# Low parts of weight chunks on GpSimd: four subtractions of 256 columns instead of one of 1024

## The chip, the cores and the metric

The kernel runs on one core of one Trainium2 chip. The metric is the device time of one execution in microseconds (us). The core has engines that run side by side, each with its own queue of instructions: TensorE (PE, with its weight loads shown as PEld), VectorE (DVE), ScalarE (ACT), GpSimd (POOL), and SyncE (SP), which here issues the loads.

## The reference

Two transformer-like layers follow each other on 256 tokens of width 2048, in float32. What matters here is the first one: a normed input is multiplied by a wide weight matrix, its columns feed three branches (a banded attention, a recurrent branch, an attention over a memory), and the branches are gated, projected and added.

```python
h = rms_norm(x, norm_g)
proj = h @ w_in
(aq, ak, av, az, br, bk, bv, bz, bwd, bad, cq, cz, ga, gb, gc) = jnp.split(proj, offsets, axis=-1)
ya = chunked_band_attention(aq, ak, av, a_rel_bias) * jax.nn.silu(az)
yb = rwkv7_time_mix(br, bk, bv, bwd, bad, ...) * jax.nn.silu(bz)
m = rms_norm(mem, mem_norm_g)
mk, mv = jnp.split(m @ w_mem_kv, 2, axis=-1)
yc = memory_cross_attention(cq, mk, mv) * jax.nn.silu(cz)
merged = sigmoid(ga) * (ya @ w_up_a) + sigmoid(gb) * (yb @ w_up_b) + sigmoid(gc) * (yc @ w_up_c)
x = x + merged @ w_o
```

The second layer has the same shape (attention, gated linear attention, a short convolution) and ends in a feed-forward block of width 5632.

## The kernel before

Each large product is done in split form. A weight chunk `w` of 128 partitions by 1024 columns (512 KB) is loaded by SP; ScalarE writes its rounded high part `wh` (line 163); the low part `wl = w - wh` is written by one subtraction of 1024 columns, on GpSimd or on VectorE (line 167). The activations lie as high and low parts too. `gemm_B` multiplies eight slices of 128 columns of each chunk: per slice one matmul of `wh` with 512 columns of activations and one of `wl` with 256 columns. `gemm_A` uses the chunk the other way round, as two slices of 512 columns, each read by two matmuls with `wl` and four with `wh`. There are four `w` buffers, three of `wh` and three of `wl`.

Which engine makes `wl` is a counter's doing. `share[0]` starts at 0.0 (all on VectorE, while the memory's keys and values are made), is 0.7 from line 334 to line 765 (seven of ten on GpSimd: the rest of the first layer up to the end of its branches), and is 0.0 again for all that follows. So GpSimd makes 161 chunks, all of 1024 columns, whose starts lie between 105.3 and 941.7 us; VectorE makes the other 802.

In that stretch TensorE works on two things at once: the weight products (the normed input against `w1A` and `w1B`), and the small matmuls of the recurrent branch (tiles `pk`, `G`, `Z`, `D`, `ch`, `oT`, `ptk`) and of the attentions (`sc`, `pt`, `po`). Between these small matmuls lie chains of short VectorE, ScalarE and GpSimd instructions of 256 columns or so: in `rwkv_inputs` the inverse square root (lines 242 to 244), `kk` (498), `k` (501), `t` (503) and the block-diagonal copies (508 to 513); in `rwkv_inverse` `lt`, `tt`, `Z`; in `rwkv_chain` `X` (599), `U` (602) and `S` (613); in the softmax `tp` (653); in the gates 669 and 677. GpSimd itself does a few of them (lines 482, 511, 514, 536, 538, 612, 633). At the end of the stretch the branch outputs `raw` are split into `yhl` by 24 pairs of instructions (lines 218 and 219, called from line 767).

The order of the instructions on each engine's queue is fixed when the kernel is built. The framework (`TileContext(nc, schedule_with_timeline_sim=True)`) chooses it by playing the program through with its own estimates of each instruction's duration, so a changed instruction can change the order around it. `rwkv_inputs`, `rwkv_inverse`, `rwkv_chain` and the fillers (the gates, the attention heads, the merge gates done ahead) are written in an order by hand, which this planner follows as their inputs allow.

Of the kernel before, what the change touches and what calls it, by code (L numbers as in the profile page):

```python
# [8 lines left out]
F32 = mybir.dt.float32  # L9
# [91 lines left out]
def _body(tc, a, out):  # L101
    nc = tc.nc
# [53 lines left out]
    share = [0.0]  # L156
    turn = [0]

    def wchunk(src, nel):
        w = wp.tile([128, 1024], F32, tag="w", name="w")  # L160
        nc.sync.dma_start(w[:, :nel], src)
        wh = whp.tile([128, 1024], F32R, tag="wh", name="wh")
        nc.scalar.copy(wh[:, :nel], w[:, :nel])  # L163
        wl = wlp.tile([128, 1024], F32R, tag="wl", name="wl")
        turn[0] += 1
        eng = nc.gpsimd if turn[0] * share[0] % 1.0 < share[0] else nc.vector
        eng.tensor_sub(wl[:, :nel], w[:, :nel], wh[:, :nel].bitcast(F32))  # L167
        return wh, wl

    def gemm_B(wd, act, kt=KD, m=128):  # L170

        ps = psg.tile([128, 512], F32, tag="g", name="g")
        for k0, kn in (chunks(kt) if m == 128 else [(0, kt)]):
            src = wd[128 * k0 * m:128 * (k0 + kn) * m].rearrange("(p c) -> p c", p=128)
            wh, wl = wchunk(src, kn * m)
            for j in range(kn):
                k = k0 + j
                mm(ps[:m, :], wh[:, j * m:(j + 1) * m], act[:, k, :], start=(k == 0), stop=False)
                mm(ps[:m, 256:512], wl[:, j * m:(j + 1) * m], act[:, k, 0:256], start=False, stop=(k == kt - 1))
        return ps  # L180

    def gemm_A(wd, act, kt=KD, ahead=None):

        ps = [psg.tile([128, 512], F32, tag="g", name="g") for _ in range(2)]
        for k0 in range(0, kt, 2):
            if ahead:
                ahead(k0)
            src = wd[128 * k0 * 512:128 * (k0 + 2) * 512].rearrange("(p c) -> p c", p=128)
            wh, wl = wchunk(src, 1024)
            for j in range(2):  # L190
                k = k0 + j
                for tt in range(2):
                    hi = act[:, k, tt * 128:(tt + 1) * 128]
                    lo = act[:, k, 256 + tt * 128:256 + (tt + 1) * 128]
                    h_ = wh[:, j * 512:(j + 1) * 512]
                    l_ = wl[:, j * 512:(j + 1) * 512]
                    mm(ps[tt], hi, h_, start=(k == 0), stop=False)
                    mm(ps[tt], hi, l_, start=False, stop=False)
                    mm(ps[tt], lo, h_, start=False, stop=(k == kt - 1))
        return ps  # L200
# [658 lines left out]
    for h in range(4):  # L859
# [23 lines left out]
        for cp in range(2):  # L883
            sl = slice(cp * 128, cp * 128 + 128)
# [176 lines left out]
```

## Time and profile before

| | |
|---|---|
| Time, median of 3 runs | 2996.11 us (2993.2 to 2996.36) |
| The profiled execution | 2997.74 us |
| Its span, first to last instruction | 2996.0 us |
| Mean granted TensorE clock | 0.992 of full speed |
| TensorE busy | 2935.0 us, 98% of the span |
| VectorE busy | 1966.4 us, 66% |
| ScalarE busy | 1439.8 us, 48% |
| GpSimd busy | 591.8 us, 20% |

The span is what the rows below cover; 1.74 us of the profiled execution lie around it. "Busy" is time with at least one instruction in work on that engine; an instruction that has been started and is held up counts as busy too.

### The profile page before, as it was taken

The numbers are of one execution on the slowest core, as the hardware profiler recorded it, in microseconds if no ns is written. First come the engines' busy times: TensorE is split into PE (matmuls) and PEld (weight loads), VectorE is DVE, ScalarE is ACT, GpSimd is POOL, SyncE is SP. The second block draws the span as 40 slices with busy tenths as digits, with TensorE's granted clock in tenths as the row PEclk, the third lists the DMA queues.
The fourth block names the chain that finished last, engine by engine and source line by source line (L and its number), as shares of the span: only waits on it lengthen the run. The fifth ranks groups of instructions, "written<-read, shape, count | busy, mean of one in ns | idle before, by whom it ended". The sixth has DMA issues, their size and how long they took to land.

```text
span 2996.0 us, 43985 instructions
## 1 busy us (share of the span) xinstructions
PE 2935.0 (98%) x16704; PEld 2575.3 (86%) x16704; DVE 1966.4 (66%) x3086; ACT 1439.8 (48%) x2174; POOL 591.8 (20%) x441
## 2 busy tenths in 40 slices
PE   8999999999999999999999999999999999999998
PEld 6888788888887888888888888888888888888887
DVE  6655687767656755666766776666676666666554
ACT  5544454444445544555445444444555444444443
POOL 6465455555564100100000000000000000000000
PEclk9999999999999999999999999999999999999999
DMA  7643233434345655665454555555555555555664
GB/s 254 198 145 133 97 117 132 142 127 135 125 150 188 222 190 190 204 198 173 153 168 164 189 190 190 190 190 190 184 196 188 190 191 191 190 190 186 189 189 148
DMA packets 151252, 522.42 MB, mean 174 GB/s; under 512 B 17200, under 2 KB 22320, under 8 KB 151040
## 3 DMA queue, kind: packets, MB, share of 16 engines
q1 hardware_dynamic: 148208, 512.72, 52.4%
q0 software_dynamic: 1824, 4.98, 0.4%
q8 instruction: 131, 2.15, 0.3%
q10 hardware_dynamic: 1008, 1.90, 0.2%
q14 instruction: 81, 0.66, 0.1%
HBM read 514.56 MB, written 4.98 MB: 173 GB/s over the span
## 4 chain that ended last, share of the span: by engine, by line
PE 81%; DVE 5%; issue 1%; ACT 1%; POOL 1%; DVEq 0%; ACTq 0%; POOLq 0%
PE g L153 76%; PE ch L153 1%; PE G L153 1%; PE oT L153 1%; POOL wl L167 1%; PE D L153 1%; PE Z L153 0%; DVE tt L568 0%; DVE wl L167 0%; PE po L153 0%; PE sc L153 0%; DVE tA L241 0%; PE glo L153 0%; DVE atrt L508 0%; DVE raw L677 0%
## 5 line engine op out<-in xcount | busy, mean ns | idle before, releaser
L153 PE MATMUL g<-xg,wh 128*128 128x512 f32 x4640 | 1636.2, 393 | 1.2 <-ACT wh L163 1.2
L163 ACT CAST wh<-w 128x1024 fp32r<-128x1024 f32 (+1 forms) x963 | 1004.3, 1043 | 1270.7 <-PE g L153 673.9
L167 DVE TENSOR_TENSOR wl<-w,wh 128x1024 fp32r<-128x1024 f32 (+1 forms) x802 | 983.1, 1226 | 718.4 <-ACT wh L163 716.5
L153 PE MATMUL g<-xg,wl 128*128 128x256 f32 x4640 | 1319.9, 285 | 6.5 <-POOL wl L167 6.5
L153 PEld LDWEIGHTS g<-xg,wh 128*128 128x128 f32 x4640 | 872.3, 188 | 179.6 <-ACT wh L163 1.8
L153 PEld LDWEIGHTS g<-xg,wl 128*128 128x128 f32 x4640 | 877.6, 189 | 9.6 <-POOL wl L167 7.4
L167 POOL TENSOR_TENSOR wl<-w,wh 128x1024 fp32r<-128x1024 f32 x161 | 395.5, 2460 | 233.2 <-ACT wh L163 212.6
L153 PE MATMUL g<-yhl,wh 128*128 128x512 f32 x768 | 269.8, 390 | 0.0
L153 PE MATMUL g<-wh,xg 128*128 128x512 f32 x768 | 250.9, 402 | 0.4 <-ACT va L318 0.4
L153 PE MATMUL g<-act,wh 128*128 128x512 f32 x704 | 244.1, 390 | 0.0
L153 PE MATMUL g<-yhl,wl 128*128 128x256 f32 x768 | 216.6, 282 | 0.0
L153 PE MATMUL g<-act,wl 128*128 128x256 f32 x704 | 198.5, 282 | 0.0
L785 POOL TENSOR_TENSOR accm<-accm,z 128x256 f32<-128x256 f32 x64 | 52.5, 820 | 654.1 <-DVE z L784 654.1
L153 PEld LDWEIGHTS g<-yhl,wh 128*128 128x128 f32 x768 | 144.2, 188 | 30.9 <-issue 0.3
L153 PEld LDWEIGHTS g<-wh,xg 128*128 128x128 f32 x768 | 143.8, 189 | 31.1 <-ACT va L318 0.5
L204 ACT COPY et<-g 128x256 f32<-128x256 f32 (+1 forms) x434 | 158.3, 365 | 6.4 <-PE g L153 6.4
L153 PE MATMUL g<-wl,xg 128*128 128x512 f32 x384 | 156.3, 407 | 1.6 <-DVE wl L167 1.6
L153 PEld LDWEIGHTS g<-act,wh 128*128 128x128 f32 x704 | 132.2, 188 | 27.7
L153 PEld LDWEIGHTS g<-yhl,wl 128*128 128x128 f32 x768 | 145.2, 189 | 0.0
L153 PEld LDWEIGHTS g<-act,wl 128*128 128x128 f32 x704 | 133.1, 189 | 0.0
L207 DVE TENSOR_TENSOR z<-g,et 128x256 f32<-128x256 f32 x216 | 90.4, 418 | 21.5 <-ACT et L204 21.0
L153 PE MATMUL g<-wh,mem_hl 128*128 128x512 f32 x256 | 84.2, 411 | 7.7 <-ACT wh L163 7.7
(348 smaller groups left out, 2964.0 us busy)
## 6 DMA issues: line engine op xcount, KB each, us to landing
w<-w2B SPq DMA_DIRECT2D x208, 512.0 KB, 3.4
w<-w1B SPq DMA_DIRECT2D x194, 512.0 KB, 3.5
w<-w_gate SPq DMA_DIRECT2D x88, 512.0 KB, 3.3
w<-w_ffup SPq DMA_DIRECT2D x88, 512.0 KB, 3.3
w<-w1A SPq DMA_DIRECT2D x64, 512.0 KB, 3.3
w<-w_down SPq DMA_DIRECT2D x64, 448.0 KB, 3.4
w<-w_mem SPq DMA_DIRECT2D x32, 512.0 KB, 4.5
w<-w_o SPq DMA_DIRECT2D x32, 512.0 KB, 4.3
```

Of the source, the lines that this page charges most:

```text
L153: nc.tensor.matmul(dst, lhsT=lhsT, rhs=rhs, start=start, stop=stop)
L163: nc.scalar.copy(wh[:, :nel], w[:, :nel])
L167: eng.tensor_sub(wl[:, :nel], w[:, :nel], wh[:, :nel].bitcast(F32))
L204: nc.scalar.copy(t[:m], ps[:m, 256:512])
L207: nc.vector.tensor_add(z[:m], ps[:m, 0:256], t[:m])
L785: nc.gpsimd.tensor_add(accm, accm, u)
```

## The change

The subtraction of a chunk that goes to GpSimd is cut into pieces of 256 columns, four instructions for 1024 columns. Chunks that go to VectorE stay as they were, and so does the count that picks the engine.

```diff
         turn[0] += 1
-        eng = nc.gpsimd if turn[0] * share[0] % 1.0 < share[0] else nc.vector
-        eng.tensor_sub(wl[:, :nel], w[:, :nel], wh[:, :nel].bitcast(F32))
+        if turn[0] * share[0] % 1.0 < share[0]:
+            for c in range(0, nel, 256):
+                sl = slice(c, c + 256)
+                nc.gpsimd.tensor_sub(wl[:, sl], w[:, sl], wh[:, sl].bitcast(F32))
+        else:
+            nc.vector.tensor_sub(wl[:, :nel], w[:, :nel], wh[:, :nel].bitcast(F32))
         return wh, wl
```

## Rows read from the trace of the kernel before

**Rows 1.** The page's first part: busy time, share of the span, instructions.

```profile
PE 2935.0 (98%) x16704; PEld 2575.3 (86%) x16704; DVE 1966.4 (66%) x3086; ACT 1439.8 (48%) x2174; POOL 591.8 (20%) x441
```

**Rows 2.** Windows: PE, PEld, DVE, ACT, POOL busy; clock, DMA share, GB/s.

```profile
75.00:950.00 875.00, 840.02 (x4836) 734.28 (x4836) 593.48 (x1082) 396.31 (x608) 481.95 (x300) 0.98 0.42 139
950.00:2996.00 2046.00, 2031.56 (x11622) 1791.82 (x11621) 1324.88 (x1942) 1001.17 (x1500) 63.35 (x91) 1.00 0.57 187
```

**Rows 3.** Waits of PE, 75 to 950 us: total, times, longest.

```profile
PE pk L153 <- DVE t L503: 8.3, 6, 3.6
PE g L153 <- POOL wl L167: 6.5, 3, 5.3
PE ch L153 <- DVE U L602: 4.1, 2, 3.4
...
PE g L153 <- ACT wh L163: 1.2, 1, 1.2
PE ch L153 <- DVE S L613: 1.1, 1, 1.1
```

**Rows 4.** Timeline around 843 us, POOL, DVE and PE: start, duration.

```profile
842.58 2.41 POOL L167 TENSOR_TENSOR wl<-w,wh 128x1024 fp32r<-128x1024 f32 x1
...
842.70 2.38 DVE L653 TENSOR_SCALAR tp<-tp,sm 128x128 f32<-128x128 f32 x1
...
845.14 0.44 PE L150 MATMUL pt<-con,tp 128*128 128x128 f32 x2 [1.38 <-DVE tp L653]
```

**Rows 5.** Timeline around 916 us, POOL and DVE.

```profile
915.75 2.41 POOL L167 TENSOR_TENSOR wl<-w,wh 128x1024 fp32r<-128x1024 f32 x1
...
918.11 2.60 POOL L167 TENSOR_TENSOR wl<-w,wh 128x1024 fp32r<-128x1024 f32 x1
...
915.78 2.65 DVE L669 SCALAR_TENSOR_TENSOR z<-et,z 128x256 f32<-128x256 f32 x1 [0.49 <-ACT et L668]
```

**Rows 6.** Groups of DVE by shape, 75 to 950 us.

```profile
L222 DVE SCALAR_TENSOR_TENSOR xg<-ld,par,xg 128x256 fp32r<-128x256 f32 x16 | 6.8, 482 | 0.0
```

**Rows 7.** Groups of POOL by shape: busy us, mean ns, idle before.

```profile
L167 POOL TENSOR_TENSOR wl<-w,wh 128x1024 fp32r<-128x1024 f32 x161 | 395.5, 2460 | 233.2 <-ACT wh L163 212.6 <-issue 7.5 <-PE G L153 6.6
...
L536 POOL TENSOR_TENSOR lt<-lt,con 128x256 f32<-128x256 f32 x16 | 11.8, 735 | 27.4 <-DVE lt L533 27.4
```

**Rows 8.** Timeline around 24 us, POOL and DVE, POOL in short instructions.

```profile
23.30 0.92 POOL L293 TENSOR_TENSOR acc<-acc,sq 128x256 f32<-128x256 f32 x1
24.18 0.79 POOL L289 TENSOR_TENSOR sq<-ld 128x256 f32<-128x256 f32 x1
24.94 1.71 POOL L293 TENSOR_TENSOR acc<-acc,sq 128x256 f32<-128x256 f32 x1
...
23.54 0.96 DVE L222 SCALAR_TENSOR_TENSOR mem_hl<-ld,par,mem_hl 128x256 fp32r<-128x256 f32 x1
24.43 1.63 DVE L167 TENSOR_TENSOR wl<-w,wh 128x1024 fp32r<-128x1024 f32 x1
```

**Rows 9.** Timeline around 280 us, POOL, DVE and PE.

```profile
278.77 2.52 POOL L167 TENSOR_TENSOR wl<-w,wh 128x1024 fp32r<-128x1024 f32 x1
...
279.01 2.99 DVE L513 TENSOR_TENSOR kt_d<-k,cum 64x256 f32<-64x256 f32 x2
...
283.27 0.49 PE L153 MATMUL ch<-btok 128*128 128x128 f32 x1 [3.42 <-DVE U L602]
```

**Rows 10.** Windows, all engines as in rows 2, after a long wait.

```profile
369.40:374.00 4.60, 4.60 (x15) 4.27 (x16) 4.48 (x12) 0.00 (x0) 1.47 (x4) 0.50 0.42 143
```

**Rows 11.** Waits of the load queue on SP.

```profile
SPq L161 <- POOL wl L167: 595.6, 152, 16.2
```

**Rows 12.** Windows, tile wl alone: PE, PEld, DVE, POOL busy; clock, DMA.

```profile
800.00:900.00 100.00, 62.18 (x216) 40.65 (x215) 6.10 (x5) 52.14 (x23) 1.00 0.47 149
```

**Rows 13.** Timeline around 924 us, POOL and DVE.

```profile
923.82 5.75 POOL L167 TENSOR_TENSOR wl<-w,wh 128x1024 fp32r<-128x1024 f32 x1 [3.11 <-ACT wh L163]
...
920.92 6.45 DVE L219 TENSOR_TENSOR yhl<-raw,yhl 128x256 fp32r<-128x256 f32 x19
```

## The prediction

> **What bounds the kernel now.** I read the busy times first: TensorE works in 98% of the span, GpSimd in little of it [rows 1]. So a gain can come only from time in which TensorE stands still or runs slowly, and the windows say where that is: from 950 us on it stands still for 2046 - 2031.6 = 14 us in 2046 at clock 1.00, between 75 and 950 us for 875 - 840 = 35 us at a mean clock of 0.98 [rows 2]. All 161 chunks made by GpSimd lie in that second stretch, so the change touches the right one, and the most that it could give back there is 35 us of waits and what the lower clock costs, at most 0.02 x 875 = 17.5 us.
>
> Third, the waits of TensorE in that stretch. Two reasons make up almost all of the 35 us: ten rows in which it waits for a VectorE instruction (from 8.3 down to 1.1 us, 26.7 together), and one in which it waits for `wl` from GpSimd (6.5 us in three waits, the longest 5.3) [rows 3].
>
> Fourth, the timeline around these waits, to see why VectorE is late. At 842.70 a VectorE instruction on 128 columns takes 2.38 us; it ends 0.09 us after a GpSimd subtraction of 1024 columns that began just before it, and TensorE starts on its result right behind it, after 1.38 us of standing still [rows 4]. At 915.78 the same: 2.65 us, ending 0.27 us after the subtraction [rows 5]. While GpSimd runs a chunk, a VectorE instruction that reads SBUF stands until the end of it. An instruction of twice that width takes 0.48 us when left alone [rows 6].
>
> **The change, part by part.**
>
> *1. Shorter holds: VectorE gets in between.* What an instruction of 256 columns on GpSimd takes is shown: 0.735 us, against 2.46 for 1024 [rows 7]. Whether VectorE gets its turn between two GpSimd instructions that follow each other at once is shown too: of the two chunks at 915.75 and 918.11 the second is recorded as started before the first has ended, yet the VectorE instruction at 915.78 is done at 918.43, and the second chunk takes 2.60 instead of 2.41 [rows 5]. And where GpSimd already works in instructions of 256 columns, the two engines take turns: at 23.30 and 24.18 GpSimd needs 0.92 and 0.79 us, and the VectorE instruction at 23.54 needs 0.96 [rows 8], where the same form alone needs 0.48 [rows 6]. So a VectorE instruction that meets quarters is held up by about 0.96 - 0.48 = 0.5 us, each time, instead of once per chunk for 1.9 to 2.2 us (2.38 and 2.65 less 0.48 [rows 4 to 6]), say 2.0.
>
> That splits the 26.7 us in two. Where one VectorE instruction stood in the way (`tp`, `tt`, `X`, `Z`, `raw` and others, eight rows, 26.7 - 8.3 - 4.1 = 14.3 us), 2.0 becomes 0.5, a saving of three quarters: 10.7 us. Where TensorE waits at the end of a long run of such instructions, the run meets every quarter: at 279.01 four copies of the lines 513 and 512 stood in front of `U`, the first two taking 2.99 us, 2.0 more than twice 0.48 [rows 6, 9]; with quarters each of the four is held for 0.5, which is 2.0, the same. The rows of `t` and `U` (12.4 us) are mostly such runs. I take 15% of them, 1.9 us; bounds are nothing, and three quarters (9.3).
>
> *2. The first quarter is there sooner.* The first matmul with `wl` needs the first 128 columns alone, there after 0.735 us instead of 2.46 [rows 7]: 1.7 us sooner. Of the three waits for `wl` the long one (5.3) gives 1.7, the other two (1.2 together) all they have: 2.9 us. No row shows that the framework lets a matmul start on a part of a tile that four instructions write; if it holds it until all is written, `wl` is ready after 4 x 0.735 = 2.94 us, 0.48 later than now, and this term becomes a loss of 3 x 0.48 = 1.4.
>
> *3. The clock.* Behind the long waits the granted clock is at the lower of its two levels: behind the longest wait for `t` (3.6 us [rows 3]) it was 0.50, which is 1.2 GHz, from 369.4 to 374 us [rows 10], a loss of 2.3 us. Up to 17.5 us go that way in the stretch [rows 2]. The longest waits (3.6, 5.3) get shorter but don't all vanish, so I take a third: 6 us, bounds nothing and 17.5.
>
> *4. What it costs.* Each chunk now keeps GpSimd for 4 x 0.735 = 2.94 us, 0.48 more; 161 chunks make 77 us [rows 7]. GpSimd is busy for 482 of the 875 us [rows 2], so the 393 idle ones take it. But 300 - 161 = 139 other GpSimd instructions stand in the same queue [rows 2, 7] (`kk` of line 511, `lt`, `tt`, `Sd`, `raw`, all links of the recurrent branch), and where one is behind a chunk it comes 0.48 us later. Chunks hold GpSimd for 395.5 of 875 us [rows 2, 7], 0.45, so it is 139 x 0.45 x 0.48 = 30 us of lateness over all these links. TensorE has other matmuls to do in most of that time, so I charge a third, 10 us; bounds are nothing and 30.
>
> "GPSIMD Engine Reference" in the Trainium skill, section "Instruction dispatch", speaks against small instructions: each pays a software dispatch of some tens of cycles. Taking 50 cycles of 1.2 GHz, three more per chunk would be an estimated 0.125 us, 20 us over all instead of the 77 that the rows give, and term 4 would shrink in that proportion from 10 to 2.6 us, the sum below from -11.5 to -18.9. The sum goes by the rows.
>
> The buffer `w` is also released later by the same 0.48 us, and SP's loads wait for that 152 times, 595.6 us in all [rows 11]. This costs nothing as long as the load has slack; the cover is that TensorE's waits for `wh`, which the loads feed, come to 1.2 us in the stretch [rows 3]. A wait of the load that grew by 0.48 us 152 times would be 73 us without this cover.
>
> *5. The order of the queues.* 483 more instructions go through the planner, which may put the small matmuls and their chains elsewhere, on any engine. No row prices that. The 35 us of waits are the outcome of one such order in some twenty places; I take nothing, with a bound of a quarter of it, 9 us, to either side.
>
> **The sum.** -10.7 - 1.9 - 2.9 - 6 + 10 = -11.5 us. The profiled execution took 2997.74 us, so 2986.2; the median of the runs lies 1.6 us below it, so 2984.6 against 2996.1. A measurement of this kernel tells about 0.2%, 6 us, from no change.
>
> **Rivals.**
>
> *All runs are long ones.* If VectorE always has the next instruction ready when a quarter ends, it is held four times for 0.5 us instead of once for 2.0, and nothing is won in term 1 or of the clock. For it speaks the place at 279 [rows 9], against it the place at 843, where one instruction stands between GpSimd and TensorE [rows 4]. Then 15% of 26.7, 4.0, and 2.9 of `wl` stand against a cost between nothing and 10: -7 to +3, or 2989 to 2999, around 2994.
>
> *GpSimd becomes the bound (slower).* Taking turns costs GpSimd too: a quarter takes 0.92 us beside an instruction of 256 columns, and 1.71 beside one of 1024 [rows 8]. Three and one of these are 4.5 us per chunk. Between 800 and 900 us GpSimd makes 23 chunks [rows 12], and its other instructions need (482 - 395.5)/875, a tenth of the time [rows 2, 7]; so above 90/23 = 3.9 us per chunk from its first start to its last end, TensorE waits for `wl`. At 4.5 it is 23 x 4.5 + 10 - 100 = 13 us late in that stretch, and with 3 us won elsewhere the time is 3006. A burst of VectorE can do the same to a quarter: at 923.82 a chunk stood for 3.3 us while 19 subtractions of line 219 ran without giving way [rows 13], and a chunk in quarters can be cut off by such a run in its middle. Against it: quarters without company make 2.94 us.
>
> *No handover between quarters (slower).* If the four run as one hold, VectorE stands for 2.94 instead of 2.46, a fifth longer: 0.2 x 26.7 = 5 us more, and 2.9 less for `wl`: with some of term 4, around 3003. The pair at 915.75 speaks against it [rows 5].
>
> *More than I think.* All eight rows vanish and most of the clock comes back: -14.3 - 6.5 - 12 + 6 = -27, 2969.
>
> **How the numbers follow.** The forecast gets 0.50 (its own range 2975 to 2992), the larger gain 0.11, all long runs 0.20, GpSimd as the bound 0.13, no handover 0.06. The range leaves out the larger half of the slow cases and what is beyond the large gain: 2968 to 3004. Faster by over 0.2% (under 2990): most of the forecast (0.47), the larger gain (0.11), a little of the long runs (0.03): 0.61. Slower by over 0.2% (over 3002): 0.11 of GpSimd as the bound, 0.04 of no handover, 0.03 from a worse order: 0.18. The rest is 0.21.
>
> **What would show it.** VectorE groups of the stretch whose means are now lifted by single long holds should drop towards 0.42 to 0.96 us, with none above 2 us. TensorE's waits for VectorE should fall from 26.7 to about 14, its idle time in the stretch from 35 to about 20, and the mean clock rise. The quarters should take 0.73 to 0.95 us, GpSimd's busy time in the stretch some 77 us more. The prediction is wrong if quarters run without VectorE in between, if TensorE waits for `wl` more than now, if the new order opens waits elsewhere, or if long runs are held for as much as before.

## The result and the profile after

The changed kernel takes 2968.03 us (median of 4 runs, 2967.79 to 2969.45) against 2996.11 before: 28.1 us less, a ratio of 0.9908 [0.9897, 0.992]. That lies 0.03 us inside the low end of the forecast's range, and 16.6 us under the forecast itself.

The page's first part, for the row of [rows 1]:

```profile
span 2966.1 us, 44553 instructions
PE 2923.9 (99%) x16704; PEld 2569.2 (87%) x16704; DVE 1933.4 (65%) x3086; ACT 1440.7 (49%) x2174; POOL 684.7 (23%) x924
```

The span fell from 2996.0 to 2966.1, by 29.9 us. TensorE's busy time fell by 2935.0 - 2923.9 = 11.1 us for the same 16704 matmuls, so those ran faster; what is left, 18.8 us, is standing still: 61.0 us before, 42.2 after. VectorE's busy time fell by 33 us for the same 3086 instructions, and GpSimd's rose by 93. The mean granted clock rose from 0.992 to 0.995, which is worth some 0.003 x 2980 = 9 of the 11.1 us (with three digits, give or take 3).

Windows, columns as in [rows 2] (the second ends with the shorter span):

```profile
75.00:950.00 875.00, 859.38 (x5006) 754.35 (x5005) 580.27 (x1111) 413.96 (x637) 584.35 (x789) 0.99 0.45 147
950.00:2966.00 2016.00, 2001.31 (x11449) 1766.29 (x11447) 1303.99 (x1912) 983.39 (x1468) 53.80 (x85) 1.00 0.58 186
```

Between 75 and 950 us TensorE stands still for 15.6 us, where it was 35.0, and gets 170 more matmuls done; after 950 us it stands still for 14.7 us, as before. So all of the gain is made in the stretch in which GpSimd makes chunks. GpSimd is busy for 584 of the 875 us there, 102 more.

Waits of TensorE, 75 to 950 us (total, times, longest), all of the list but four rows:

```profile
PE g L153 <- DVE wl L171: 3.5, 1, 3.5
PE ch L153 <- DVE U L606: 3.3, 2, 1.8
PE pt L150 <- DVE tp L657: 2.8, 1, 2.8
PE ch L153 <- DVE S L613: 2.5, 1, 2.5
PE Z L153 <- DVE gm L539: 0.9, 1, 0.9
...
PE pk L153 <- DVE t L507: 0.2, 1, 0.2
```

`wl` from GpSimd (6.5 us in [rows 3]) is gone from the list, and `t` (8.3 us) all but gone. The rows with VectorE, the ones left out among them, come to 14.8 us, against 26.7.

VectorE, groups by shape in the stretch (busy us, mean ns of one). Before:

```profile
L677 DVE SCALAR_TENSOR_TENSOR raw<-z,raw 128x256 f32<-128x256 f32 x16 | 18.8, 1177 | 0.4
L503 DVE SCALAR_TENSOR_TENSOR t<-r,par,k 128x256 f32<-128x256 f32 x8 | 9.3, 1168 | 0.2
L653 DVE TENSOR_SCALAR tp<-tp,sm 128x256 f32<-128x256 f32 x8 | 4.7, 587 | 0.2
```

and after (lines are 4 higher):

```profile
L681 DVE SCALAR_TENSOR_TENSOR raw<-z,raw 128x256 f32<-128x256 f32 x16 | 9.7, 608 | 0.3
L657 DVE TENSOR_SCALAR tp<-tp,sm 128x256 f32<-128x256 f32 x8 | 8.8, 1095 | 0.1
L507 DVE SCALAR_TENSOR_TENSOR t<-r,par,k 128x256 f32<-128x256 f32 x8 | 5.6, 695 | 0.1
```

The mean of `raw` halves and that of `t` falls by two fifths. Counted over all records of the stretch, reciprocals and VectorE's own chunks left out, 44 VectorE instructions last longer than 1.9 us before, and 4 after. The mean of `tp` rises instead; one single instruction does that, and the last section shows it.

GpSimd's chunks, the group that answers to the first of [rows 7]:

```profile
L169 POOL TENSOR_TENSOR wl<-w,wh 128x256 fp32r<-128x256 f32 x644 | 494.1, 800 | 174.4 <-ACT wh L163 158.2 <-PE D L153 7.9 <-issue 5.6
```

and the load queue's wait for them, which answers to [rows 11]:

```profile
SPq L161 <- POOL wl L169: 453.9, 150, 6.9
```

A chunk costs 494.1 / 161 = 3.07 us of GpSimd's time instead of 2.46, and the loads wait for it less, not more.

How quarters and VectorE share their turns, timeline around 895 us, GpSimd and VectorE:

```profile
896.06 0.92 POOL L169 TENSOR_TENSOR wl<-w,wh 128x256 fp32r<-128x256 f32 x1
896.94 0.92 POOL L169 TENSOR_TENSOR wl<-w,wh 128x256 fp32r<-128x256 f32 x1
...
895.42 0.96 DVE L223 TENSOR_TENSOR yhl<-raw,yhl 128x256 fp32r<-128x256 f32 x1
896.30 0.96 DVE L223 TENSOR_TENSOR yhl<-raw,yhl 128x256 fp32r<-128x256 f32 x1
```

Each engine gets one instruction in between two of the other: 0.92 and 0.96 us each, as in [rows 8]. A whole chunk would have stood in VectorE's way for some 2.4 us [rows 4, 5].

### The profile page after: what moved, and what is told of

It reads as the page before. It is cut to its first block, busy times and chain, and to the rows that moved or that the text cites. A ratio compares the mean times of both kernels' runs of the same rounds, so it can differ in the third digit from the quotient of the medians.

```text
span 2966.1 us, 44553 instructions
## 1 busy us (share of the span) xinstructions
PE 2923.9 (99%) x16704; PEld 2569.2 (87%) x16704; DVE 1933.4 (65%) x3086; ACT 1440.7 (49%) x2174; POOL 684.7 (23%) x924
## 4 chain that ended last, share of the span: by engine, by line
PE 93%; DVE 4%; POOL 1%; ACT 1%; issue 1%; DMA 0%; SPq 0%; DVEq 0%; ACTq 0%; POOLq 0%
PE g L153 86%; PE D L153 1%; PE ch L153 1%; PE oT L153 1%; PE G L153 1%; PE Z L153 1%; PE sc L153 1%; PE po L153 1%; POOL acc L297 1%; POOL sq L293 0%; POOL wl L169 0%; PE ptk L150 0%; DVE yhl L223 0%; PE glo L153 0%; ACT wh L163 0%
## 5 line engine op out<-in xcount | busy, mean ns | idle before, releaser
L169 POOL TENSOR_TENSOR wl<-w,wh 128x256 fp32r<-128x256 f32 x644 | 494.1, 800 | 174.4 <-ACT wh L163 158.2
```

Of the source, the lines that this page charges most:

```text
L169: nc.gpsimd.tensor_sub(wl[:, sl], w[:, sl], wh[:, sl].bitcast(F32))
```

## The experiments

The theory was the one of the forecast: the length of a single GpSimd instruction is what VectorE, and behind it TensorE, pays for. Its rivals: the new order of the queues made the gain; the earlier first quarter made it; the choice of chunks did. Times of before on the chips used for these runs lie between 2996.0 and 2997.0 us.

**Cut in the old order.** The queues are planned with whole chunks, as before; then each subtraction of 1024 columns is replaced where it stands, by four of 256. The first has its waits, the last its signal.

```diff
+for k in range(n):                      # n = 4
+    new.append(piece(i, k * w, w, waits if k == 0 else [], updates if k == n - 1 else []))
```

> The order of all queues is that of the kernel before; only each GpSimd subtraction of 1024 columns is replaced, in its place, by four of 256, of which the first has the waits and the last the signal, so nobody can use the first quarter early. If the gain comes from the shorter holds of VectorE, most of it stays: 2996 less some 12 us of waits and 6 to 8 us of clock, so 2974 to 2982. If it comes from the order that the planner chose anew, or from the first quarter being there sooner, nothing is won and each chunk is 0.5 us later: 2996 to 3003.

Measured: 2972.36 us, 0.9919 [0.9905, 0.9932]. Of the 28.1 us, 24.2 come without any change of order and without an earlier first quarter. TensorE's waits for VectorE in the stretch come to 13.6 us, against 26.7.

**Whole in the new order.** The reverse: the queues of the changed kernel, with its four instructions per chunk in their places, but the first does 1021 columns and the other three one column each.

```diff
+at, n = (0, 1021) if k == 0 else (1020 + k, 1)
```

> The order of all queues is that of the changed kernel; of the four subtractions of a chunk the first does 1021 columns and the other three one column each, so VectorE is held for a whole chunk again. If the gain comes from the shorter holds: back to 2990 to 3000. If it comes from the new order: 2968 to 2973, as after the change.

Measured: 2998.1 us, 1.0006 [0.9997, 1.0015]: the whole gain is gone. This kernel's window of the stretch, columns as in [rows 2]:

```profile
75.00:950.00 875.00, 839.44 (x4848) 733.40 (x4847) 597.22 (x1081) 396.92 (x606) 585.96 (x783) 0.99 0.43 139
```

and the first waits of TensorE there:

```profile
PE ch L153 <- DVE U L606: 8.4, 3, 3.4
PE g L153 <- DVE wl L171: 5.3, 3, 3.1
PE Z L153 <- DVE gm L539: 2.5, 1, 2.5
PE pk L153 <- DVE t L507: 2.5, 4, 1.0
PE pt L150 <- DVE tp L657: 2.4, 1, 2.4
```

GpSimd is busy for 586 us, as long as in the changed kernel (584), with the same instructions in the same order. What differs is how long one of them lasts, and TensorE stands still for 35.6 us again, behind VectorE above all. Together with the run before, this shows the length of the single instruction as the cause of those 24.2 us. Against the 2996.59 us of before beside it this run is 1.5 us slower (-0.9 to +4.5), so the new order and GpSimd's longer work together cost no more than that.

**Late release.** The changed kernel, but the signals of the first three quarters are given together with the fourth's (for 158 of the 161 chunks, those whose quarters stand together on the queue). It prices the earlier first quarter.

```diff
+updates = []                            # quarters 1 to 3
+if o.offset == 768: updates = [all four signals as one, update_value=sum(...)]
```

> The changed kernel with its order, but the signal of the first three quarters of a chunk is given with the fourth, where the four stand together on the queue, so that TensorE starts on a chunk only when all of it is there. If the early first quarter is worth what the prediction put on it (2.9 us and more), 2971 to 2976. If it is not, 2968 to 2970.

Measured: 2972.48 us, 0.9923 [0.9909, 0.9936], 4.4 us above the changed kernel. TensorE's waits in the stretch:

```profile
PE g L153 <- POOL wl L169: 7.4, 6, 3.3
PE ch L153 <- DVE U L606: 3.3, 2, 1.8
PE pt L150 <- DVE tp L657: 2.8, 1, 2.8
PE ch L153 <- DVE S L613: 2.5, 1, 2.5
```

The wait for `wl` from GpSimd is back, and the VectorE rows `U`, `tp` and `S` are the same to the digit (the wait for VectorE's own `wl` fell from 3.5 to 1.4). So the early quarter is worth some 4.4 us. That is less than the 6 us that the forecast counts as no change, and the two intervals overlap; but none of the five runs (2971.24 to 2974.86) reaches into the four of the changed kernel (2967.79 to 2969.45), and the 7.4 us of waits show where it comes from. This run and the first experiment cut alike and, but for three chunks, release alike; they differ in order: 2972.48 and 2972.36 us. So no gain from the order shows.

**Two halves, and eights.** As in the first experiment, in the old order, with `n = 2` and with `n = 8`.

> The order of the kernel before, each GpSimd subtraction cut in its place into two of 512 columns, signal with the second. A half should take about 1.3 us. If what counts is the longest hold of VectorE, half a chunk gives roughly half of what four pieces gave in the same order (24 us): 2982 to 2988. If any gap in which VectorE can slip through is enough, most of it: 2972 to 2978.

> The order of the kernel before, each GpSimd subtraction cut in its place into eight of 128 columns, signal with the eighth. A piece takes 0.51 us as in the run of eight pieces planned anew, a chunk 4 us. If that run lost against four pieces because chunks come later and GpSimd is busy for 80% of the stretch, this one loses too: 2978 to 2986. If it lost by an unlucky order of the planner alone: 2966 to 2973.

Measured: halves 2984.61 us, 0.996 [0.9947, 0.9972], a gain of 12.3; eights 2992.96 us, 0.9991 [0.9982, 0.9999], a gain of 4. Halves give half of what quarters gave, and TensorE's waits for VectorE lie between too: 26.7 us with whole chunks, 20.0 with halves, 13.6 with quarters, all in the old order. Eights miss what was expected. Their group on GpSimd:

```profile
L167 POOL TENSOR_TENSOR wl<-w,wh 128x128 fp32r<-128x128 f32 x1288 | 607.6, 508 | 109.5 <-ACT wh L163 94.7 <-issue 11.3 <-DVE ss L353 1.0
```

the window of the stretch:

```profile
75.00:950.00 875.00, 842.57 (x4876) 731.81 (x4875) 550.06 (x1088) 399.99 (x614) 690.19 (x1428) 0.99 0.42 141
```

and TensorE's first wait there:

```profile
PE g L153 <- POOL wl L167: 12.9, 17, 2.0
```

A chunk now takes 607.6 / 161 = 3.8 us of GpSimd, which is busy for 79% of the stretch, and TensorE waits for `wl` 17 times. This is the rival "GpSimd becomes the bound", a little before the 3.9 us per chunk at which the forecast put it; quarters, at 3.1, stay clear of it. It isn't all: one VectorE instruction (`z` of line 669, at 903.75) stands for 11.82 us through 27 GpSimd instructions in a row.

**Eights, planned anew.** The change itself, with 128 in the place of 256, so that each eighth also signals for itself.

```diff
-            for c in range(0, nel, 256):
-                sl = slice(c, c + 256)
+            for c in range(0, nel, 128):
+                sl = slice(c, c + 128)
```

> Eight pieces of 128 columns, planned anew. A piece should take about 0.45 us (0.735 for 256 columns, 2.46 for 1024, so 0.16 fixed), a chunk 3.6 us. If what is left of VectorE's holds still costs TensorE time, it shrinks further: 2962 to 2968. If GpSimd, busy for three quarters of the stretch by then, becomes the bound, or its later links cost: 2970 to 2985.

Measured: 2978.57 us, 0.994 [0.9927, 0.9952]. GpSimd is busy for 701 of the 875 us, TensorE waits for its `wl` 7 times, 6.0 us in all. That is 14.4 us better than eights in the old order, so early release and a plan that knows of the eights, which this run doesn't separate, win a good part back, but still 10.5 us behind the quarters of the change. Here the waits for VectorE count for more, 18.4 us, and 12.3 of them stand behind VectorE instructions that a long row of eighths held up. Timeline of the worst, VectorE, GpSimd and TensorE:

```profile
452.19 7.80 DVE L369 TENSOR_TENSOR tA<-zr 128x256 f32<-128x256 f32 x1
...
456.39 3.33 POOL L169 TENSOR_TENSOR wl<-w,wh 128x128 fp32r<-128x128 f32 x8
...
460.25 0.58 PE L153 MATMUL ch<-X,ttf 128*128 128x128 f32 x1 [5.26 <-DVE X L603]
```

So eights lose in two ways: GpSimd is late with its chunks, and now and then VectorE doesn't get its turn for longer than with quarters (up to 10.56 and 11.82 us, against 5.73). No run tells the two apart.

**Other chunks.** The counter that picks the engine starts at 5 instead of 0, so that other chunks go to GpSimd (163 of them); once with whole chunks, once cut.

```diff
-    turn = [0]
+    turn = [5]
```

> The kernel before with the counter that shares out the chunks started at 5, so that other chunks go to GpSimd and the planner makes another order. If the waits are the outcome of chunks of 2.4 us falling upon VectorE's chains wherever they stand, about the same time: 2988 to 3004. If the order before was an unlucky one: well below 2988.

> The changed kernel with the same counter started at 5. If the shorter holds are the cause, it is 20 to 34 us faster than its partner with whole chunks: 2960 to 2982. If the 28 us were one order's luck, the gap is under 10 us.

Measured: whole 2999.14 us, 1.0009 [1.0, 1.0018]; cut 2970.87 us, 0.9914 [0.99, 0.9927]. Cutting gains 28.3 us here too: it is no luck of the places in which the chunks fell. In the cut one TensorE does wait for `wl` from GpSimd once, for 4.9 us: a quarter stood for 5.47 us beside a run of line 223 on VectorE.

**Another share.** The changed kernel with the counter's share set to 0.5, 0.6, 0.8 and 0.3 instead of 0.7.

```diff
-        share[0] = 0.7
+        share[0] = 0.5
```

> The changed kernel with five of ten chunks on GpSimd instead of seven. GpSimd's time falls by about 45 chunks of 3.1 us, VectorE's rises by 45 of 1.23. If what is left of the waits comes from GpSimd's holds and its late chunks, 2956 to 2965. If VectorE, whose chains then stand behind more whole chunks of 1024 columns of its own, is what TensorE waits for: 2970 to 2985.

> Six of ten chunks on GpSimd. Between the changed kernel and the run with five of ten: 2960 to 2968 if fewer chunks on GpSimd help, 2968 to 2978 if they don't.

> Eight of ten chunks on GpSimd, which is then busy for some 78% of the stretch. If GpSimd's own load sets in as it did with eight pieces: 2975 to 2990. If VectorE's freed time counts for more: 2960 to 2968.

> The changed kernel with three of ten chunks on GpSimd. If GpSimd's holds and late chunks are what is left, a little under the run with five of ten: 2958 to 2964. If VectorE's own whole chunks now stand in front of its chains: 2966 to 2980.

| Share set | Chunks on GpSimd | Time (us) | Ratio to before |
|---|---|---|---|
| 0.3 | 78 | 2967.44 | 0.9904 [0.9887, 0.9921] |
| 0.5 | 103 | 2964.48 | 0.9894 [0.9879, 0.9909] |
| 0.6 | 156 | 2972.91 | 0.9923 [0.991, 0.9935] |
| 0.7 (the change) | 161 | 2968.03 | 0.9908 [0.9897, 0.992] |
| 0.8 | 168 | 2976.17 | 0.9933 [0.9921, 0.9946] |

The second column is counted in each trace, and it shows that the setting isn't the share. By the kernel's formula the five counts come out together only if 206 chunks pass the counter, so 161 are 78%, not seven of ten. The test `turn * share % 1.0 < share` compares rounded products: where 0.6 x turn should leave exactly 0.6, it sometimes leaves a little less and counts as a hit. So 0.6, 0.7 and 0.8 are nearly the same split, and the differences among them are not a trend with GpSimd's load. One wait is more than the whole loss at 0.6: TensorE stands still for 7.87 us, until 920.76, for two quarters that take 4.67 us while VectorE runs its subtractions of line 223 and two chunks of its own. At 0.8 it waits for no chunk from GpSimd, but 23.4 us for VectorE, two of whose instructions stand for 5.5 and 6.1 us through nine GpSimd instructions each.

From 78 to 161 chunks, GpSimd is busy for 332 to 584 us of the stretch, and the two ends are 0.6 us apart, with 0.6 alone above both. With quarters its load hardly matters in that span. No run had all chunks on VectorE.

## Why the prediction came out as it did

The sign and the main mechanism were right, the size was not: -28.1 us against -11.5. That is the number of the rival "more than I think" (2969), though not its parts, since the eight rows that were to vanish kept 11.3 of 14.3 us. That the time still fell inside the range, by 0.03 us, was luck: three terms erred to the same side. By its terms:

| Term | Forecast | Measured in the profile |
|---|---|---|
| 1. Waits of TensorE for VectorE | -12.6 | -11.9 (26.7 to 14.8) |
| 2. The first quarter sooner | -2.9 | -6.5 (the whole row; -4.4 by the late release) |
| 3. Clock | -6 | -9 to -11 |
| 4. GpSimd slower per chunk | +10 | with term 5 at most +4.5 (whole in the new order: +1.5) |
| 5. Order | 0 | 0 (late release against cut in the old order) |

**Term 4 is the one that failed**, with 10 of the 16.6 us. It multiplied the 0.48 us by the 139 other GpSimd instructions and charged a third. The lengthening was there (0.6 us a chunk, 102 us in the stretch), but no wait of TensorE for a GpSimd result is left in the list above, the waits of the loads fell instead of rising [rows 11], and the whole chunks in the new order, with the same GpSimd time, are only 1.5 us slower than before. GpSimd is idle for 290 us of the stretch, which can cover it; no run isolates that. The price exists further on: eights, at 3.8 us a chunk, brought it in as waits for `wl`, near the 3.9 us that the rival had worked out. So a cost under cover should have been charged nothing up to that point; a share of it was not a middle way. It is nothing in this order: with other chunks and with a share of 0.6, late quarters kept TensorE waiting for 4.9 and 7.9 us.

**Term 2 was sized too small.** The forecast let the long wait of 5.3 us lose only the 1.7 us of the first quarter itself. All 6.5 went. The late release brings back 7.4 us of waits for `wl` and 4.4 us of time, so most of it is this term.

**Term 3 was sized too small** by 3 to 5 us: TensorE's busy time fell by 11.1 us, and the mean clock says 9. The profile shows the lower level behind waits after the change too: the clock was 0.63 from 531.4 to 536 us, behind the wait of 2.8 for `tp`, so much of that stretch at 1.2 GHz. That shorter waits alone brought it back isn't shown: with a share of 0.5, two runs with the same program had 0.992 and 0.995.

**Term 1 was right in its sum and wrong in its parts**, which is luck too: the errors cancelled. The rows of `t` and `U` went from 12.4 to 3.5 us (5.7 in the old order), where 1.9 less was forecast; the other VectorE rows went from 14.3 to 11.3 (7.9), where they were to lose 10.7. The argument from [rows 9], that a run of VectorE instructions meets every quarter, holds at its own place. The cut in the old order, around 275 us, VectorE and TensorE:

```profile
272.73 1.81 DVE L513 TENSOR_TENSOR kt_d<-k,cum 64x256 f32<-64x256 f32 x2
274.57 1.70 DVE L512 TENSOR_TENSOR bt_d<-kk,cum 64x256 f32<-64x256 f32 x2
...
276.65 0.58 PE L153 MATMUL ch<-btok 128*128 128x128 f32 x1 [3.08 <-DVE U L602]
```

Each of the four copies is held, and the wait for `U` is 3.08 us instead of 3.42. In the changed kernel the copies stand free, but the quarters meet the run in front of them, and TensorE waits 2.52 us for `S` there. What was wrong is that `t` belonged to the long runs: in front of its long waits of before, one instruction had been held for the length of a chunk (`t` itself for 2.56 us at 366.75, line 243 for 2.50 at 448.03), and that is what quarters shorten.

The eight other rows were read too simply. Of the instructions named in them, `tt`, `X`, `Z` and `S` are not held themselves; mostly one in front of them on VectorE's queue is. Before, GpSimd, VectorE and TensorE:

```profile
390.49 2.55 POOL L167 TENSOR_TENSOR wl<-w,wh 128x1024 fp32r<-128x1024 f32 x1
390.84 2.48 DVE L677 SCALAR_TENSOR_TENSOR raw<-z,raw 128x256 f32<-128x256 f32 x1
393.25 0.28 DVE L599 COPY X<-ch 128x128 f32<-128x128 f32 x1
393.58 0.38 PE L153 MATMUL ch<-X,ttf 128*128 128x128 f32 x1 [1.59 <-DVE X L599]
```

Nor does every VectorE instruction that reads SBUF stand until the chunk's end, as the forecast had it. Of those that started with over 1.2 us of a chunk still to run, all 8 of `z` of line 669 and all 6 of `raw` of line 677 stood (1.80 and 2.44 us in the mean), but none of the 27 of `z` of line 207 did, which take one input from a matmul's result and one from SBUF (0.42 us). The eight rows kept more than forecast also because three new or longer waits stand among them: `wl` of VectorE itself (3.5: its chunk starts at 901.08, behind sixteen subtractions of line 223 that began at 892.44), `tp` (2.8) and `S` (2.5).

Of the signs that were named: holds over 2 us all but vanished (44 to 4 over 1.9), waits for VectorE fell to 14.8 (14 forecast), idle time to 15.6 (20), the quarters took 0.80 in the mean (0.73 to 0.95), and GpSimd's busy time grew by 102 us (77). The last is more than forecast because the mean of a quarter includes turns taken, which the 0.735 of [rows 7] did not.

"GPSIMD Engine Reference" in the Trainium skill, section "Instruction dispatch", stood beside term 4 with an estimated 0.125 us per chunk. The trace shows more for the three added instructions: the four quarters at 528.26 below, which ran undisturbed, span 530.31 + 0.71 - 528.26 = 2.76 us, 0.35 more than the 2.41 of a whole chunk [rows 4]. The measurement decides.

## What to carry to other kernels

Where a helper engine's long instructions hold up short ones on the engine that feeds the bottleneck, cut them: the hold is mostly one instruction long, so halves gave 12 us, quarters 24 and, with the early first quarter, 28. Stop before the fixed cost of the pieces fills the helper: with eights it was busy for 79% and the gain fell to 4, or 18 when planned anew with early signals. Look in the trace for instructions whose recorded time is several times that of their form when alone and that end with the other engine's; the one that the bottleneck waits for may only stand behind such a one. Price a helper's extra work at nothing while its idle time covers it, but say at what length per piece of work the cover ends. And count in the trace what a setting did before reading a trend from it.

## What was not expected of the hardware

The turn between two GpSimd instructions isn't always handed over. Timeline of the changed kernel from 526 us, VectorE, GpSimd and TensorE:

```profile
526.00 5.18 DVE L657 TENSOR_SCALAR tp<-tp,sm 128x256 f32<-128x256 f32 x1
...
526.30 0.75 POOL L540 TENSOR_TENSOR lt<-lt,con 128x256 f32<-128x256 f32 x1
527.01 1.29 POOL L542 TENSOR_TENSOR tt<-tt,con 128x512 fp32r<-128x512 f32 x1
528.26 0.72 POOL L169 TENSOR_TENSOR wl<-w,wh 128x256 fp32r<-128x256 f32 x1
...
530.31 0.71 POOL L169 TENSOR_TENSOR wl<-w,wh 128x256 fp32r<-128x256 f32 x1
...
531.42 0.72 PE L150 MATMUL pt<-con,tp 128*128 128x128 f32 x3 [2.79 <-DVE tp L657]
```

One VectorE instruction stood through six GpSimd instructions in a row, which ran at 0.71 us a quarter, as if alone, and TensorE waited 2.79 us for it. It is this one that lifted the mean of `tp`. Long VectorE instructions of the same kind start at 163.47 (`lml`, 5.73 us), 705.33 (`z`, 2.76) and 882.45 (`gq`, 5.29): four in the stretch, so the rival "no handover" does happen, a few times. With eights planned anew there are eight over 1.9 us, the longest 10.56. The reverse is there too: at 901.41 one quarter lasted 4.16 us while VectorE ran a chunk of its own and subtractions of line 223 without giving way, which is what [rows 13] showed before the change. "SBUF — State Buffer" in the Trainium skill, section "Who interferes with whom", says that a VectorE instruction with two inputs in SBUF contends with a GpSimd instruction that reads SBUF, and of VectorE's two-port modes that whoever issues first has the shared pair of ports for its whole instruction and the other blocks fully. The holds of `lml`, `z` and `gq` agree. What decides who is next between two instructions stays open, and no run here was made for it.

The granted clock also differs between runs of one program. The kernel with a share of 0.5 took 2969.28 us at a mean clock of 0.992 and 2964.29, 2964.64 and 2964.31 at 0.995; in the first, the profiled one, TensorE stood still for only 12.9 us in the stretch, less than in the changed kernel, with a clock of 0.98 there. So less standing still didn't mean more clock; why is open.
